# Hybrid decoder layer, fp32 weights in two halves: the halves of some stages start at other bytes of SBUF

## Chip, cores and metric

The kernel runs on one core of one Trainium2 chip. The metric is the device time of one execution in microseconds (us); the median before is 1079.64 us, from two runs of 1079.58 and 1079.71.

## What is computed

One layer on 256 tokens of width 2048, all in float32. Cut to what matters here:

```python
h   = rmsnorm(x)
z   = h @ w_in          # pool channels | q | k | v | indexer q | indexer k | indexer weights
A   = pool_mixer(z)     # four groups, causal means over 2, 4, 8, 16 tokens, a small matmul each
B   = dsa_attention(z)  # 16 indexer heads, causal top-64 keys, 8 heads of softmax attention
x1  = x + concat(A, B) @ w_out                     # 2048 x 2048
up  = rmsnorm(x1) @ w_up                           # 2048 x 11264
out = x1 + (silu(gate(conv3(up))) * val(conv3(up))) @ w_down    # 5632 x 2048
```

## The kernel before, in words

**Two halves.** To reach float32 accuracy with the fast fp32r matmul, every operand is split into a high and a low half, and each product is three matmuls: high by high, high by low, low by high (`mm_tok`, L225 to L227, and `mm_feat`, L231 to L233). The weights stream in as pieces of 1 MB units (`raw`, two buffers). For each piece of 1024 columns ScalarE rounds `raw` into `whi` (L118) and VectorE subtracts it into `wlo` (L119); `whi` and `wlo` have four buffers each. The activations are held in halves for a whole stage: `xhl` (normalised input), `yhl` (mixer output), `x2hl` (second norm, in the memory of `xhl`) and `ghl` (FFN gate product).

**Stages.** TensorE goes through one list of 384 pieces. First the columns of `w_in` in chunks in the order of `ORDER`: indexer chunks i0, i1, i2, key k0, k1, pool u0, query q0, q1, u1, value v0, u2, v1, u3. Then `w_out` (32 pieces), `w_up` (176 pieces) and `w_down` (88 pieces). In the token chunks (i, k, q, v: `tok_chunk`, `mm_tok`) the activation slice of 128 tokens is the stationary operand and the weights are the moving one, of 400, 384, 320 or 512 columns. In the pool chunks and in everything after (`mm_feat`) it is the other way round: 128 columns of weight halves are stationary and the 256 tokens of an activation half move. The four pool chunks have 384 such matmuls (96 each); k, q and v have six chunks of 96 matmuls of 512 columns; `w_out` has 768, `w_up` 4224, `w_down` 2112, which is 264 for each eighth (11 pieces of 24).

**Side work.** Indexer scores, top-k, attention heads, pooling and norms are put between the pieces by a table of steps (`at(step, f)`): before piece n's matmuls the units of piece n+3 are loaded, piece n+2 is split, and the side functions of step n are recorded. The order on each engine is then that of the recording, but for instructions that wait for a buffer: such a one is put behind what frees it. Head h's probabilities are transposed into `pT` (L528, five buffers) at step 60+3h and used in `att_pv` at step 74+h for heads 0 to 3, and later for 4 to 7. The sums for the second norm are kept in `sq1` (L610, own memory); `ffn_open` (L631) closes the memory pool of the mixer and opens that of the FFN at step G0+1; `r2.cols` (L167) and `r2.rows` (L178) are the small matmuls of the second norm.

**Where the operands lie.** The starts of the tiles, in bytes of a partition, are fixed in the compiled program. A stationary weight slice is 128 columns of 4 bytes, 512 bytes; a moving activation half is 1,024 bytes and a moving slice of 512 columns 2,048. So in a stage the remainder of an operand's start by 512 bytes is the same for every matmul, and this text counts it in steps of 64 bytes, as a **place** from 0 to 7. Before: `whi` and `wlo` all start at multiples of 512 (91,648 and so on): place 0. `xhl` starts at 34,560: place 4. `x2hl` is 448 bytes further: place 3. `yhl` (136,832 and 64 of offset) and `ghl` (124,416 and 192): place 3. The offsets are those of `PLACE` (L45, in elements of 4 bytes). The **distance** of a stage is the place of the moving operand less that of the stationary one, modulo 8:

| stage | moving | stationary | distance before | after |
|---|---|---|---|---|
| i0, first and second slice of a piece | weights 0 and 1 | xhl 4 | 4 and 5 | 4 and 5 |
| i1, both slices | weights 0 | xhl 4 | 4 | 4 |
| i2, first and second slice | weights 0 and 4 | xhl 4 | 4 and 0 | 4 and 0 |
| k0, k1, q0, q1, v0, v1 | weights | xhl 4 | 4, all six | 7, 1, 2, 6, 3, 5 |
| u0 to u3 | xhl 4 | weights | 4 | 3 |
| w_out, w_up | yhl, x2hl 3 | weights 0 | 3 | 3 |
| w_down, eighths 0 to 7 | ghl 3 | weights | 3, all eight | 3, 2, 1, 0, 7, 6, 5, 4 |

(The second slice of a piece of i0 starts 1,600 bytes in, of i2 1,280.)

Of the kernel before, what the change touches and what calls it, by code (L numbers as in the profile page):

```python
# [8 lines left out]
F32 = mybir.dt.float32  # L9
F32R = mybir.dt.float32r  # L10
BF16 = mybir.dt.bfloat16
# [4 lines left out]
P = 128  # L16
S = 256
# [19 lines left out]
GROUPS = (3, 2, 1, 0)  # L37

ORDER = ("i0", "i1", "i2", "k0", "k1", "u0", "q0", "q1", "u1", "v0", "u2", "v1", "u3")
WARM = 8  # L40

PLACE = {"x": 0, "x2": 112, "y": 16, "g": 48}  # L45


def placed(pool, n, name, o, of=None):

    m = n * 2 * S  # L50
    t = of[0] if of else pool.tile([P, m + (128 if name == "xhl" else o)], F32R, name=name)
    return t, t[:, o:o + m].rearrange("p (k a t) -> p k a t", k=n, a=2)
# [3 lines left out]
def hybrid_kernel(ctx, tc, xT, par, wIa, wIb, wIc, wI2, wA, wU, wP, wO, wUp, wDn, out):  # L56
    nc = tc.nc
    PS = bass.MemoryType.PSUM

    cp = ctx.enter_context(tc.tile_pool(name="cp", bufs=1))  # L60
    wp = ctx.enter_context(tc.tile_pool(name="wp", bufs=2))
# [5 lines left out]

    xhl = placed(cp, KT, "xhl", PLACE["x"])
    x2hl = placed(cp, KT, "xhl", PLACE["x2"], xhl)
    xhl, x2hl = xhl[1], x2hl[1]  # L70
    ga = cp.tile([P, KT], F32, name="ga")


    warm = cp.tile([P, 512], BF16, name="warm")
    nc.vector.memset(warm, 0.0)
    pw = ps_s.tile([P, 512], F32, name="pw", tag="ss")
    for i in range(WARM):
        nc.tensor.matmul(pw, warm[:, 0:P], warm, start=True, stop=True)

    ident = cp.tile([P, P], F32, name="ident")  # L80
    make_identity(nc, ident)
# [9 lines left out]
    class Unit:  # L91


        def __init__(self, src, n, cuts=None):
            self.src, self.n, self.raw, self.cuts = src, n, None, cuts or [(0, n)]
# [10 lines left out]
    class Piece:  # L106


        def __init__(self, unit, a, b, mm):
            self.unit, self.a, self.b, self.mm = unit, a, b, mm  # L110

        def split(self, parts=1):
            self.hi = wp.tile([P, 1024], F32R, name="whi", tag="whi", bufs=4)
            self.lo = wp.tile([P, 1024], F32R, name="wlo", tag="wlo", bufs=4)
            n = (self.b - self.a) // parts
            for c in range(0, n * parts, n):
                raw, hi = self.unit.raw[:, self.a + c:self.a + c + n], self.hi[:, c:c + n]
                i1 = nc.scalar.activation(hi, raw, AF.Copy)  # L118
                i2 = nc.vector.tensor_tensor(self.lo[:, c:c + n], raw, hi.bitcast(F32), op=ALU.subtract)  # L119
                self.issued = i1.ins, i2.ins  # L120
# [4 lines left out]
    pieces = []  # L125
    sides = {}

    def at(step, f, *a):
        sides.setdefault(step, []).append(lambda: f(*a))
# [12 lines left out]
    zc = zp.enter_context(tc.tile_pool(name="zc", bufs=1))  # L142
# [42 lines left out]
    r1, r2 = TokenNorm("r1"), TokenNorm("r2")  # L185
# [31 lines left out]
    def mm_tok(acc, piece, ks, width):  # L217

        pt = acc.get()
        for i, k in enumerate(ks):  # L220
            wh, wl = piece.get(i * width, width)
            for th in range(2):
                t = slice(th * P, (th + 1) * P)
                o = pt[:, th, :width]
                nc.tensor.matmul(o, xhl[:, k, 0, t], wh, start=(k == 0), stop=False)  # L225
                nc.tensor.matmul(o, xhl[:, k, 0, t], wl, start=False, stop=False)  # L226
                nc.tensor.matmul(o, xhl[:, k, 1, t], wh, start=False, stop=(k == KT - 1))  # L227

    def mm_feat(o, wh, wl, rhs, first, last):

        nc.tensor.matmul(o[:, 0:S], wh, rhs[:, 0], start=first, stop=False)  # L231
        nc.tensor.matmul(o[:, 0:S], wh, rhs[:, 1], start=False, stop=False)  # L232
        nc.tensor.matmul(o[:, 0:S], wl, rhs[:, 0], start=False, stop=last)  # L233

    def tok_chunk(srcs, width, cuts=()):

        acc = Acc()
        for q in range(4):
            u = Unit(srcs[q], 4 * width, cuts[q] if q < len(cuts) else None)
            for h in range(2):  # L240
                def mm(p, k0=4 * q + 2 * h):
                    mm_tok(acc, p, (k0, k0 + 1), width)
                pieces.append(Piece(u, 2 * h * width, (2 * h + 2) * width, mm))
        return acc


    def pool_chunk(n):
        acc = Acc()
        for j in range(2):
            u = Unit(wU[2 * n + j], D)  # L250
            for h in range(2):
                def mm(p, j=j, h=h):
                    pt = acc.get()
                    for i in range(8):
                        k = 8 * h + i
                        mm_feat(pt[:, j], *p.get(i * P, P), xhl[:, k], k == 0, k == KT - 1)
                pieces.append(Piece(u, h * 1024, (h + 1) * 1024, mm))
        return acc

    ia, za, ua, first = [], {}, [], {}  # L260
    W = IWIDTH[0]

    def pair_chunk():

        accs = Acc(), Acc()
        seq = [(0, 0), (0, 1)] + [cm for m in range(6) for cm in ((1, m), (0, m + 2))] + [(1, 6), (1, 7)]
        for j in range(8):
            n = [2 * IWIDTH[c] for c, m in seq[2 * j:2 * j + 2]]
            src = wIa if j == 0 else wIc if j == 7 else wIb[j - 1]
            u = Unit(src, sum(n), [(0, W), (W, 2 * W), (2 * W, 4 * W)] if j == 0 else  # L270
                     [(0, n[0]), (n[0], sum(n))] if j < 4 else None)
            for i in range(2):
                def mm(p, c=seq[2 * j + i][0], m=seq[2 * j + i][1]):
                    mm_tok(accs[c], p, (2 * m, 2 * m + 1), IWIDTH[c])
                pieces.append(Piece(u, n[0] * i, n[0] + n[1] * i, mm))
        ia.extend(accs)

    for name in ORDER:
        first[name] = len(pieces)
        if name == "i0":  # L280
            pair_chunk()
        elif name == "i1":
            first[name] = first["i0"] + 8
        elif name == "i2":
            ia.append(tok_chunk([wI2[q] for q in range(4)], IWIDTH[2]))
        elif name[0] == "u":
            ua.append(pool_chunk(int(name[1])))
        else:
            c = ("k0", "k1", "q0", "q1", "v0", "v1").index(name)
            za[name] = tok_chunk([wA[c, q] for q in range(4)], 512)  # L290


    yhl = placed(zc, KT, "yhl", PLACE["y"])[1]
    oa = [Acc() for g in range(8)]
# [26 lines left out]
    G0 = len(pieces)  # L321
# [16 lines left out]
    for i in range(16 * NF // 8):  # L338
        if i % 2 == 0:
            u = Unit(wDn[i // 2], 2048)  # L340

        def mm(p, i=i):
            for n in range(8):
                t, k = divmod(8 * i + n, NF)
                if t < 14:
                    mm_feat(da[t // 2].get()[:, t % 2], *p.get(n * P, P), ghl[:, k], k == 0, k == NF - 1)
                else:
                    mm_feat(da[t - 7].get(), *p.get(n * P, P), ghl[:, k], k == 0, k == NF - 1)
        o = (i % 2) * 1024
        pieces.append(Piece(u, o, o + 1024, mm))  # L350


    qiT = [zc.tile([P, 8, S], F32R, name=f"qiT{c}", tag="big", bufs=2) for c in range(2)]
# [169 lines left out]
    def att_pt(h):  # L523
        pe = hs[h]
        tp = ps_s.tile([P, 512], F32, name="tp", tag="ss")
        for i in range(3):
            nc.tensor.transpose(tp[:, i * P:(i + 1) * P], pe[:, i * P:(i + 1) * P], ident)  # L527
        pT = zc.tile([P, 3 * P], F32, name="pT", tag="pT", bufs=5)  # L528
        nc.scalar.activation(pT, tp[:, 0:3 * P], AF.Copy)
        hs[h] = pT  # L530

# [75 lines left out]
                                           op0=ALU.mult, op1=ALU.subtract)  # L607


    sq1 = cp.tile([P, 2, S], F32, name="sq1")  # L610

    def x1_out(jp):
        pt = oa[jp].get()
        x1 = xf[:, 2 * jp:2 * jp + 2]
        nc.vector.tensor_tensor(x1, pt[:, :, 0:S], x1, op=ALU.add)
        for j in range(2):
            split_x(2 * jp + j, x1[:, j], pr[:, C_FG:C_FG + KT], True, x2hl)
        if jp == 0:
            nc.scalar.activation(sq1, x1, AF.Square)
        else:  # L620
            t = zc.tile([P, 2, S], F32, name="xt", tag="t2", bufs=5)
            nc.scalar.activation(t, x1, AF.Square)
            nc.vector.tensor_tensor(sq1, sq1, t, op=ALU.add)
# [7 lines left out]
    def ffn_open():  # L631
        nonlocal ghl
        zp.close()
        fp = ctx.enter_context(tc.tile_pool(name="fp", bufs=1))
        ghl = placed(fp, NF, "ghl", PLACE["g"])[1]
        fw["up"] = [fp.tile([P, 2, S + 2], F32, name=f"up{i}") for i in range(2)]
# [82 lines left out]
        at(st + 2 + 4 * (n < 3), pool_mix, n)  # L719
    for jp in range(8):  # L720
        at(O0 + 4 * jp + 4, x1_out, jp)
    at(G0 + 1, ffn_open)
    at(G0 + 1, sq1_sum)
    at(G0 + 2, r2.cols, sq1[:, 0])
    at(G0 + 3, r2.diag)
    at(G0 + 4, r2.rows)
    for f in range(NF):
# [104 lines left out]
```

## Time and profile before

| | |
|---|---|
| median of two runs | 1079.64 us |
| the profiled execution | 1079.61 us |
| its span, first to last instruction | 1077.9 us |
| TensorE matmuls busy | 1072.1 us (99%), 8644 matmuls |
| TensorE weight loads busy | 1042.4 us (97%) |
| VectorE, ScalarE, GpSimd busy | 697.0, 544.9, 13.8 us |
| mean granted clock of TensorE | 0.999 |

Matmuls overlap in the profile: one of 256 columns is shown with some 277 ns, but the next starts long before that. So the **spacing**, the time from a matmul's start to the next one's, is what tells how fast the stream runs. It is read from the start times in the timeline, over 12 or more matmuls, since a start is shown to 10 ns.

### The profile page before, as it was taken

What the parts mean: (1) busy time and instruction counts of PE and PEld (TensorE: products, weight loads), DVE (VectorE), ACT (ScalarE), POOL (GpSimd) and SP (SyncE); (2) the same over time, 40 slices, a digit from 0 to 9 for tenths busy, and PEclk for the clock granted to TensorE, in tenths of its full rate; (3) what the DMA queues carried; (4) which work ended last, traced back from release to release, by engine and by line L of the source; (5) the groups of instructions that cost most, each with busy time, mean ns of one, the idle gap of its engine ahead of it and who ended that gap; (6) DMA issues with size and microseconds to landing.
All of it is one profiled execution on the core that took longest, in us unless ns stands there. A gap on an engine that the chain in (4) does not pass through costs nothing.

```text
span 1077.9 us, 20309 instructions
## 1 busy us (share of the span) xinstructions
PE 1072.1 (99%) x8644; PEld 1042.4 (97%) x8644; DVE 697.0 (65%) x986; ACT 544.9 (51%) x745; POOL 13.8 (1%) x25
## 2 busy tenths in 40 slices
PE   9999999999999999999999999999999999999998
PEld 7988989889999999999999999999999999999998
DVE  7667857765566676777777777777676544444443
ACT  7655356654545555555555555555555433333342
POOL 0001000000000000000000000000000000000000
PEclk9999999999999999999999999999999999999999
DMA  8553554444555455555555555555555555556552
GB/s 288 174 180 144 194 209 156 165 167 157 194 192 192 168 199 195 194 193 196 196 195 196 196 196 196 195 196 195 188 197 187 196 204 199 203 200 204 203 207 85
DMA packets 31770, 204.55 MB, mean 190 GB/s; under 512 B 3648, under 2 KB 4288, under 8 KB 8640
## 3 DMA queue, kind: packets, MB, share of 16 engines
q1 hardware_dynamic: 30240, 201.16, 52.9%
q10 hardware_dynamic: 1440, 2.11, 0.5%
q8 instruction: 67, 1.10, 0.4%
q14 instruction: 23, 0.19, 0.0%
HBM read 201.15 MB, written 2.10 MB: 189 GB/s over the span
## 4 chain that ended last, share of the span: by engine, by line
PE 99%; DMA 1%; SPq 0%; ACT 0%; DVE 0%; issue 0%; ACTq 0%
PE mm L233 26%; PE mm L231 26%; PE mm L232 26%; PE mm L225 6%; PE mm L227 5%; PE mm L226 5%; PE sp L413 1%; DMA xf<-in_xT_dram 1%; PE sp L499 0%; PE tp L487 0%; PE op L539 0%; PE tp L527 0%; PE tp L403 0%; PE pm L232 0%; PE pm L233 0%; PE pm L231 0%
## 5 line engine op out<-in xcount | busy, mean ns | idle before, releaser
L119 DVE TENSOR_TENSOR wlo<-raw,whi 128x1024 fp32r<-128x1024 f32 (+4 forms) x385 | 462.3, 1203 | 293.0 <-ACT whi L118 289.1
L118 ACT ACTIVATE whi<-raw 128x1024 fp32r<-128x1024 f32 (+4 forms) x385 | 400.0, 1042 | 434.6 <-PE mm L232 305.9
L231 PE MATMUL mm<-xhl,whi 128*128 128x256 f32 x1536 | 426.1, 277 | 0.0
L233 PE MATMUL mm<-xhl,wlo 128*128 128x256 f32 x1536 | 424.9, 277 | 0.0
L232 PE MATMUL mm<-xhl,whi 128*128 128x256 f32 x1536 | 424.9, 277 | 0.0
L232 PEld LDWEIGHTS mm<-xhl,whi 128*128 128x128 f32 x1536 | 288.9, 188 | 0.2
L231 PEld LDWEIGHTS mm<-xhl,whi 128*128 128x128 f32 x1536 | 288.8, 188 | 0.2
L233 PEld LDWEIGHTS mm<-xhl,wlo 128*128 128x128 f32 x1536 | 288.8, 188 | 0.0
L231 PE MATMUL mm<-ghl,whi 128*128 128x256 f32 x704 | 194.3, 276 | 0.0
L232 PE MATMUL mm<-ghl,whi 128*128 128x256 f32 x704 | 194.3, 276 | 0.0
L233 PE MATMUL mm<-ghl,wlo 128*128 128x256 f32 x704 | 194.3, 276 | 0.0
L231 PEld LDWEIGHTS mm<-ghl,whi 128*128 128x128 f32 x704 | 132.2, 188 | 0.0
L232 PEld LDWEIGHTS mm<-ghl,whi 128*128 128x128 f32 x704 | 132.2, 188 | 0.0
L233 PEld LDWEIGHTS mm<-ghl,wlo 128*128 128x128 f32 x704 | 132.2, 188 | 0.0
L225 PE MATMUL mm<-whi,xhl 128*128 128x512 f32 (+3 forms) x288 | 108.6, 377 | 1.0 <-ACT xhl L135 0.8
L226 PE MATMUL mm<-wlo,xhl 128*128 128x512 f32 (+3 forms) x288 | 106.6, 370 | 0.2 <-DVE wlo L119 0.2
L227 PE MATMUL mm<-whi,xhl 128*128 128x512 f32 (+3 forms) x288 | 106.7, 370 | 0.0
L231 PE MATMUL mm<-yhl,whi 128*128 128x256 f32 x256 | 70.8, 277 | 0.0
L232 PE MATMUL mm<-yhl,whi 128*128 128x256 f32 x256 | 70.7, 276 | 0.0
L233 PE MATMUL mm<-yhl,wlo 128*128 128x256 f32 x256 | 70.7, 276 | 0.0
L225 PEld LDWEIGHTS mm<-whi,xhl 128*128 128x128 f32 x288 | 54.2, 188 | 9.4 <-ACT xhl L135 1.1
L227 PEld LDWEIGHTS mm<-whi,xhl 128*128 128x128 f32 x288 | 54.1, 188 | 8.4 <-DVE xhl L138 0.5
(144 smaller groups left out, 751.9 us busy)
## 6 DMA issues: line engine op xcount, KB each, us to landing
raw<-in_wUp_dram SPq DMA_DIRECT2D x88, 1024.0 KB, 4.8
raw<-in_wDn_dram SPq DMA_DIRECT2D x44, 1024.0 KB, 4.8
raw<-in_wA_dram SPq DMA_DIRECT2D x24, 1024.0 KB, 4.8
raw<-in_wO_dram SPq DMA_DIRECT2D x16, 1024.0 KB, 4.8
raw<-in_wU_dram SPq DMA_DIRECT2D x8, 1024.0 KB, 4.8
raw<-in_wI_dram SPq DMA_DIRECT2D x4, 640.0 KB, 3.9
raw<-in_wIb_dram SPq DMA_DIRECT2D x3, 784.0 KB, 4.4
xf<-in_xT_dram SPq DMA_DIRECT2D x8, 256.0 KB, 5.1
```

The source lines that it names most:

```text
L118: i1 = nc.scalar.activation(hi, raw, AF.Copy)
L119: i2 = nc.vector.tensor_tensor(self.lo[:, c:c + n], raw, hi.bitcast(F32), op=ALU.subtract)
L225: nc.tensor.matmul(o, xhl[:, k, 0, t], wh, start=(k == 0), stop=False)
L226: nc.tensor.matmul(o, xhl[:, k, 0, t], wl, start=False, stop=False)
L227: nc.tensor.matmul(o, xhl[:, k, 1, t], wh, start=False, stop=(k == KT - 1))
L231: nc.tensor.matmul(o[:, 0:S], wh, rhs[:, 0], start=first, stop=False)
L232: nc.tensor.matmul(o[:, 0:S], wh, rhs[:, 1], start=False, stop=False)
L233: nc.tensor.matmul(o[:, 0:S], wl, rhs[:, 0], start=False, stop=last)
L413: nc.tensor.matmul(sp[:, a:b], q, kiT[:, e, 0:b - a], start=(e == 0), stop=(e == 1))
```

## The change

It gives each `Piece` an offset in elements. `whi` and `wlo` become 512 bytes wider, and the piece uses 1024 columns from its offset on. The offset is 16 elements (64 bytes) times a number: 1 in the pool columns; 3, 5, 6, 2, 7, 1 in k0, k1, q0, q1, v0, v1; 0 to 7 in the eighths of `w_down`; 0 in the indexer chunks, `w_out` and `w_up`. The memory for it (eight tiles by 512 bytes) comes from three places: `sq1` moves into the rotating buffers "t2" of the mixer's pool, for which `ffn_open` is recorded behind `r2.cols`; `pT` has four buffers for five; and the tile of the warm-up matmuls is half as wide, with 16 matmuls of 256 columns for 8 of 512. In the program that comes of it, all activation tiles keep their places (`yhl` starts 1,536 bytes later, `ghl` too), and so do the small ones that TensorE reads, but for `sq1`, which goes from place 6 to place 0.

```diff
-WARM = 8
+WARM = 16
+PAD = 128
...
-    warm = cp.tile([P, 512], BF16, name="warm")
+    warm = cp.tile([P, 256], BF16, name="warm")
...
-        nc.tensor.matmul(pw, warm[:, 0:P], warm, start=True, stop=True)
+        nc.tensor.matmul(pw[:, 0:256], warm[:, 0:P], warm, start=True, stop=True)
...
-        def __init__(self, unit, a, b, mm):
-            self.unit, self.a, self.b, self.mm = unit, a, b, mm
+        def __init__(self, unit, a, b, mm, off=0):
+            self.unit, self.a, self.b, self.mm, self.off = unit, a, b, mm, off
...
-            self.hi = wp.tile([P, 1024], F32R, name="whi", tag="whi", bufs=4)
-            self.lo = wp.tile([P, 1024], F32R, name="wlo", tag="wlo", bufs=4)
+            self.hi = wp.tile([P, 1024 + PAD], F32R, name="whi", tag="whi", bufs=4)[:, self.off:self.off + 1024]
+            self.lo = wp.tile([P, 1024 + PAD], F32R, name="wlo", tag="wlo", bufs=4)[:, self.off:self.off + 1024]
...
-                pieces.append(Piece(u, h * 1024, (h + 1) * 1024, mm))
+                pieces.append(Piece(u, h * 1024, (h + 1) * 1024, mm, 16))
...
-            za[name] = tok_chunk([wA[c, q] for q in range(4)], 512)
+            za[name] = tok_chunk([wA[c, q] for q in range(4)], 512, off=16 * (3, 5, 6, 2, 7, 1)[c])
...
-        pieces.append(Piece(u, o, o + 1024, mm))
+        pieces.append(Piece(u, o, o + 1024, mm, 16 * (i // 11)))
...
-        pT = zc.tile([P, 3 * P], F32, name="pT", tag="pT", bufs=5)
+        pT = zc.tile([P, 3 * P], F32, name="pT", tag="pT", bufs=4)
...
-    sq1 = cp.tile([P, 2, S], F32, name="sq1")
+    sq1 = None
...
+        if jp == 0:
+            sq1 = zc.tile([P, 2, S], F32, name="sq1", tag="t2", bufs=5)
...
-    at(G0 + 1, ffn_open)
     at(G0 + 1, sq1_sum)
-    at(G0 + 2, r2.cols, sq1[:, 0])
+    at(G0 + 2, lambda: r2.cols(sq1[:, 0]))
+    at(G0 + 2, ffn_open)
```

With four buffers, the fifth head's `pT` needs the buffer of the first head's, which is read by that head's `att_pv`. On ScalarE, at the end of chunk v0, the rows before are these (`whi` are the splits, `pT_2140` is head 4's, `pe` the exponentials of head 5, `zv` the values leaving PSUM):

```order
L490 ACTIVATE qk_2114<-tp_2109,gqk_110 128x256
L491 ACTIVATE qk_2114<-tp_2109 128x256
L455 ACTIVATE zv_2133<-mm_1886,r1_429 128x512 x2
L529 ACTIVATE pT_2140<-tp_2136 128x384
L118 ACTIVATE whi_2183<-raw_2099 128x1024
L511 ACTIVATE pe_2152,sume_2153<-sm_2145,nb_2150,sc1_1832 128x128
L511 ACTIVATE pe_2152,sume_2153<-sm_2145,nb_2150,sc1_1832 128x256
L118 ACTIVATE whi_2211<-raw_2181 128x1024
```

After, head 4's is `pT_2147`:

```order
L492 ACTIVATE qk_2121<-tp_2116,gqk_118 128x256
L493 ACTIVATE qk_2121<-tp_2116 128x256
L457 ACTIVATE zv_2140<-mm_1893,r1_436 128x512 x2
L120 ACTIVATE whi_2190<-raw_2106 128x1024
L513 ACTIVATE pe_2159,sume_2160<-sm_2152,nb_2157,sc1_1839 128x128
L513 ACTIVATE pe_2159,sume_2160<-sm_2152,nb_2157,sc1_1839 128x256
L120 ACTIVATE whi_2218<-raw_2188 128x1024
L120 ACTIVATE whi_2269<-raw_2188 128x1024
L531 ACTIVATE pT_2147<-tp_2143 128x384
```

Head 4's `pT` has moved behind two splits and the exponentials; nothing else on ScalarE has moved. On VectorE one small product (`nb`) changes places with its neighbour, and on TensorE nothing moves but the warm-up.

## Rows read from the trace of the kernel before

**Rows 1.** The page: busy time of the engines, and the granted clock in 40 slices.
```profile
PE 1072.1 (99%) x8644; PEld 1042.4 (97%) x8644; DVE 697.0 (65%) x986; ACT 544.9 (51%) x745; POOL 13.8 (1%) x25
...
PEclk9999999999999999999999999999999999999999
```
**Rows 2.** Stretches: length, busy (count) of PE, PEld, DVE, ACT, POOL, clock, DMA, GB/s.
```profile
112.00:124.00 12.00, 12.00 (x100) 11.92 (x99) 10.17 (x27) 6.29 (x9) 1.64 (x1) 1.00 0.49 175
500.00:600.00 100.00, 100.00 (x885) 100.00 (x884) 72.72 (x105) 53.98 (x74) 0.00 (x0) 1.00 0.55 191
900.00:1000.00 100.00, 100.00 (x885) 100.00 (x884) 46.83 (x41) 39.32 (x37) 0.00 (x0) 1.00 0.59 204
```
**Rows 3.** Timeline of TensorE (start us, us, line): 12 matmuls of u0.
```profile
122.23 0.28 PE L231 MATMUL mm<-xhl,whi 128*128 128x256 f32 x1
...
123.67 0.40 PE L225 MATMUL mm<-whi,xhl 128*128 128x512 f32 x1
```
**Rows 4.** The same in w_out, 12 matmuls.
```profile
311.71 0.28 PE L231 MATMUL mm<-yhl,whi 128*128 128x256 f32 x1
...
313.07 0.28 PE L231 MATMUL mm<-yhl,whi 128*128 128x256 f32 x1
```
**Rows 5.** Line 231 alone, first and eighth eighth of w_down: count, first and last start.
```profile
L231 PE MATMUL mm<-ghl,whi x88: 276/276/276, 835.1 to 864.7; 128*128 128x256 f32 x88
...
L231 PE MATMUL mm<-ghl,whi x87: 276/276/276, 1044.9 to 1074.1; 128*128 128x256 f32 x87
```
**Rows 6.** Timeline of TensorE in k1, steady: 12 matmuls.
```profile
99.92 0.39 PE L225 MATMUL mm<-whi,xhl 128*128 128x512 f32 x1
...
102.64 0.39 PE L225 MATMUL mm<-whi,xhl 128*128 128x512 f32 x1
```
**Rows 7.** Timeline of TensorE in i0: six matmuls of each slice of a piece.
```profile
17.97 0.34 PE L225 MATMUL mm<-whi,xhl 128*128 128x400 f32 x1
...
19.05 0.34 PE L225 MATMUL mm<-whi,xhl 128*128 128x400 f32 x1
...
20.14 0.34 PE L225 MATMUL mm<-whi,xhl 128*128 128x384 f32 x1
```
**Rows 8.** The same in i2.
```profile
47.76 0.31 PE L225 MATMUL mm<-whi,xhl 128*128 128x320 f32 x1
...
48.64 0.31 PE L225 MATMUL mm<-whi,xhl 128*128 128x320 f32 x1
...
49.53 0.33 PE L413 MATMUL sp<-kiT,qiT 128*128 128x128 f32 x2
```
**Rows 9.** Timeline of TensorE in k0, behind indexer scores (L413): six matmuls.
```profile
68.79 0.40 PE L225 MATMUL mm<-whi,xhl 128*128 128x512 f32 x1
...
70.18 0.40 PE L225 MATMUL mm<-whi,xhl 128*128 128x512 f32 x1
```
**Rows 10.** Timeline of TensorE in w_up, around the small matmuls of the norm.
```profile
361.47 0.28 PE L231 MATMUL mm<-xhl,whi 128*128 128x256 f32 x1
...
366.66 0.28 PE L233 MATMUL mm<-xhl,wlo 128*128 128x256 f32 x1
366.78 0.61 PE L178 MATMUL pb<-dg,ones 128*128 128x128 f32 x4
```
**Rows 11.** Timeline at the end of v0 and in u2: head 4's pT, heads 0 and 5.
```profile
212.30 0.49 ACT L529 ACTIVATE pT<-tp 128x384 f32<-128x384 f32 x1
...
217.82 1.06 ACT L118 ACTIVATE whi<-raw 128x1024 fp32r<-128x1024 f32 x1 [1.83 <-PE mm L232]
...
218.11 0.38 PE L540 MATMUL op<-pT,zv 128*128 128x128 f32 x2
...
222.29 0.49 PE L527 MATMUL tp<-ident,pe 128*128 128x128 f32 x3
```
**Rows 12.** Timeline of the start: warm-up, and what the third real matmul waits for.
```profile
1.25 3.60 PE L78 MATMUL pw<-warm 128*128 128x512 bf16 x8 [1.25 <-DVE warm L75]
...
5.42 0.19 PEld L227 LDWEIGHTS mm<-whi,xhl 128*128 128x128 f32 x1 [0.25 <-DVE xhl L138]
```

More of the change, by code (lines that the diff above doesn't have):

```diff
@@ L233, in mm_feat, with tok_chunk @@
         nc.tensor.matmul(o[:, 0:S], wl, rhs[:, 0], start=False, stop=last)
-    def tok_chunk(srcs, width, cuts=()):
+    def tok_chunk(srcs, width, cuts=(), off=0):
         acc = Acc()
@@ L242, in mm @@
                     mm_tok(acc, p, (k0, k0 + 1), width)
-                pieces.append(Piece(u, 2 * h * width, (2 * h + 2) * width, mm))
+                pieces.append(Piece(u, 2 * h * width, (2 * h + 2) * width, mm, off))
         return acc
@@ L607, in pool_mix @@
                                            op0=ALU.mult, op1=ALU.subtract)
-    sq1 = cp.tile([P, 2, S], F32, name="sq1")
+    sq1 = None
     def x1_out(jp):
+        nonlocal sq1
+        if jp == 0:
+            sq1 = zc.tile([P, 2, S], F32, name="sq1", tag="t2", bufs=5)
         pt = oa[jp].get()
```

## The prediction
> **What bounds the kernel now.** I read the page's list of engines first: TensorE's matmuls fill 1072.1 us of a span of 1077.9, at the full granted clock of 2.4 GHz in nearly all of it, while VectorE and ScalarE have 65% and 51% [rows 1]. So only what changes TensorE's own stream can change the time. The table by stretch comes next, and what to see in it is that the stream does not care how busy the others are: with VectorE at 73 us of 100 and at 47 us of 100 the same 885 matmuls touch a stretch [rows 2]. That leaves the spacing of the matmuls. A matmul of 256 columns at 2.4 GHz has 256 / 2.4 = 106.7 ns of columns to stream, one of 512 has 213.3.
>
> The timeline gives the spacings. In the pool chunk u0, 12 matmuls take 123.67 - 122.23 = 1.44 us, 120.0 ns each [rows 3]. In `w_out` the same 12 take 1.36 us, 113.3 ns each [rows 4], and in `w_down` 261 matmuls take 29.6 us in the first eighth and 258 take 29.2 in the last, 113.4 and 113.2 ns [rows 5]. The instructions have the same shapes, and VectorE's load was just ruled out; what differs is the distance of moving and stationary operand: 4 in the pool chunks, 3 in the others. So distance 4 costs 13.3 ns over the columns and distance 3 costs 6.7, half of it.
>
> In the token chunks the roles are exchanged. In k1 the spacing is 2.72 us / 12 = 226.7, 13.3 over the columns, at distance 4 [rows 6]. i0 has two distances in each piece: six matmuls of 400 columns take 1.08 us at distance 4 (180.0 each, 13.3 over) and 1.09 at distance 5 (181.7, 15.0 over) [rows 7]. i2 has distances 4 and 0: 0.88 and 0.89 us for six of 320 columns, some 147 to 148 each, 13 to 15 over [rows 8]. So with the roles exchanged 4 and 0 cost the same as 4 in the pool chunks, and 5 no less. Distances 1, 2, 6 and 7 are shown nowhere, in either role.
>
> **The change part by part.** The profiled execution took 1079.61 us, 1.71 more than its span and 0.03 under the median, so sums on it are sums on the median.
>
> *Pool columns.* All 384 matmuls go from distance 4 to 3: 384 x (120.0 - 113.3) = 2.56 us less [rows 3, 4]. This is the term I trust most, since w_out shows the same kind of matmul at the new distance.
>
> *Key, query, value chunks.* 96 matmuls in each, so one step of 6.7 ns is worth 0.64 us in a chunk. v0 comes to distance 3: if what holds in `w_out` holds with the roles exchanged, -0.64. v1 comes to 5, which i0 shows 1.7 ns dearer than 4: +0.16 [rows 7]. k0, k1, q0, q1 come to 7, 1, 2, 6, unseen: from -0.64 (as distance 3) to +0.46. The upper end is the dearest spacing that rows of these chunks show, behind an interruption: 1.39 us for six, 231.7 ns, 5 over the steady 226.7, times 96 = 0.48 [rows 9]. As the nearer rows give 4, 0 and 5 all alike, I take -0.32 for each of the four, halfway to distance 3: -1.28. Sum of the six: -1.76; ends -3.84 (all as good as 3) and +2.9 (all as dear as rows 9).
>
> *w_down.* 264 matmuls in each eighth, so a step of 6.7 ns is worth 1.76 us. Eighth 0 stays as it is. Eighth 7 comes to distance 4, which u0 shows: +1.76. Eighths 1 to 6 come to 2, 1, 0, 7, 6, 5. The nearest rows at both sides are the two steady levels of this shape, 113.3 and 120.0; 0 and 5 are dear with the roles exchanged [rows 7, 8], 1, 2, 6, 7 are open. I take the middle, +0.88 each, +5.28 together. Sum +7.04. The ends: nothing can go under 106.7 ns of columns, so no eighth gains more than 1.76, so six such gains and the +1.76 of eighth 7 make -8.8; all seven at 120 make +12.3.
>
> *The rest costs nothing that ends anything.* `whi` and `wlo` are written and read by the same instructions of the same sizes on ScalarE and VectorE, which have a third and a half of the span free [rows 1]. With a buffer less, head 4's `pT` waits for head 0's last matmul, at 218.11 + 0.38 = 218.49 instead of running at 212.30; ScalarE is then in a split until 218.88, so `pT` ends near 219.4. What is behind it on ScalarE, a `yhl` and a `qk`, comes 0.4 us later; the first matmul that can need the freed PSUM buffer is head 5's transpose at 222.29, so 2.9 us of cover are left [rows 11]. Without that cover it would cost the wait itself, at most the 6.9 us by which `pT` moves. The warm-up has the same 4,096 columns and ends where the third real matmul still waits for VectorE at 5.42 [rows 12]. `sq1` and the later `ffn_open` touch VectorE, ScalarE and GpSimd only.
>
> *Sum:* -2.56 - 1.76 + 7.04 = +2.7 us, 1079.6 + 2.7 = 1082.3 us.
>
> *A rule that speaks against all of it.* The rows show a spacing that goes with the place of the operands [rows 3, 4]. The Trainium skill, "TensorE: Matmul & The Clock Gate", Step-by-step: what each phase is for, has two independent SBUF read ports for TensorE, so that loading the next weights takes no bandwidth from the running matmul; "SBUF — State Buffer", Who interferes with whom, adds that TensorE never waits on anyone. By that rule no place matters; it is the first rival. The Trainium skill, "TensorE: Matmul & The Clock Gate", Back-to-back issue gap, gives 256 / 2.4 + 2.5 = 109.2 ns as the spacing of such a matmul alone; no stretch here reaches it, and if a distance did, an eighth would gain 1.1 us by that estimate.
>
> **The rivals.**
>
> *No place matters* (the rule above). Then u0's 120 has another reason, for example its neighbours in the side work, every term is 0, and the time is 1079.6. For it: the pool chunks are also the ones with pooling and attention between their pieces. Against it: within 12 matmuls without any side work the spacing is steady at 120 [rows 3], and k1 shows the same 13.3 ns without pool columns [rows 6].
>
> *Only distance 4 is dear, all the others are as good as 3.* Then pool -2.56, k to v -3.84, w_down +1.76: -4.6, 1075.0. For it: 3 is good right beside 4. Against it: 0 and 5 in i2 and i0 are as dear as 4 [rows 7, 8].
>
> *Distance 3 is the only good one.* Pool -2.56, v0 -0.64, w_down +12.3: +9.1, 1088.7. For it: i0 and i2. Against it: those have the roles exchanged.
>
> *A slow rhythm sets in for good; slower by over 2%.* At distance 3 there is a second rhythm. From 361.47 to 366.66 the spacing is 5.19 us over 44 matmuls, 118.0 ns, behind the norm's small matmuls, and it lasts until the next of these at 366.78, behind which it is 113.3 to the end [rows 10, 5]. Here `sq1` has another place and the offsets come on top; if the stream falls into this rhythm behind the second small matmul (366.78) instead, nothing interrupts it any more. The remaining 4224 - 96 = 4128 matmuls of `w_up` and 2112 of `w_down` would pay 4.7 ns: +29.3, less 2.56: 1106.3, +2.5%. It decides at one point, the first matmuls behind 366.78. Against it: there the addresses and the order are those of before.
>
> **How the numbers follow.** Mixture of the two levels, my forecast, 1082.3: 0.50, with a range of its own from 1077 to 1087. No place matters, 1079.6: 0.12. Only 4 is dear, 1075.0: 0.15. Only 3 is good, 1088.7: 0.19. Slow rhythm, 1106.3: 0.04. The range reaches from just under the 1075.0 to just over the 1088.7 and leaves out the slow rhythm and the gains below both levels: 1074.5 to 1090. Against the bound of 2%, 21.6 us, about what a measurement of this kernel can tell from no change, only the slow rhythm is slower: 0.04. Faster by that much would need every matmul of `w_down`, k, q and v at the bare columns and more: 0.01. Within: 0.95.
>
> **What would show it right or wrong.** In the profile after: u0 at 113.3 ns a matmul; v0 at 220 for 512 columns; eight stretches of `w_down` with different spacings, from 29.9 us (113.3) to 31.7 us (120.0) each, the last at 31.7; the spacing in `w_out` and `w_up` unchanged at 113.3; no gap of TensorE at 218 to 223 us. Wrong if u0 stays at 120 (then place is not it), if all eighths are alike, if a spacing lies outside 106.7 to 120, or if `w_up` runs at 118 behind 367 us.

## The result, and the profile after

The changed kernel takes 1088.13 us (two runs, 1088.01 and 1088.25) against 1079.64: a ratio of 1.0078, interval 1.0062 to 1.0094. It is 0.8% slower, within the 2% that the forecast called no change, and within its range of 1074.5 to 1090; the forecast itself, 1082.3, is 5.8 us too low.

The profiled execution after took 1088.01 us, with a span of 1086.3 (1077.9 before). The page's list of engines and the granted clock, for [rows 1]:

```profile
PE 1081.1 (100%) x8652; PEld 1050.8 (97%) x8652; DVE 696.3 (64%) x986; ACT 545.5 (50%) x745; POOL 13.7 (1%) x25
...
PEclk9999999999999999999999999999999999999999
```

TensorE's busy time grew by 9.0 us, with VectorE and ScalarE within 0.7 us of before, and the clock is still 2.4 GHz. The eight added matmuls are those of the warm-up (16 halves for 8). So the same matmuls stand further apart. The next view is the one that answers to [rows 5]: line 233 of the changed kernel (line 231 before) alone, in each eighth of `w_down`. Columns: count, shortest, median and longest duration in ns, first and last start in us.

```profile
L233 PE MATMUL mm<-ghl,whi x88: 276/276/276, 834.8 to 864.4; 128*128 128x256 f32 x88
...
L233 PE MATMUL mm<-ghl,whi x88: 276/281/285, 864.7 to 895.7; 128*128 128x256 f32 x88
...
L233 PE MATMUL mm<-ghl,whi x88: 279/279/284, 896.0 to 926.8; 128*128 128x256 f32 x88
...
L233 PE MATMUL mm<-ghl,whi x88: 280/283/287, 927.1 to 958.4; 128*128 128x256 f32 x88
...
L233 PE MATMUL mm<-ghl,whi x88: 276/276/279, 958.8 to 988.4; 128*128 128x256 f32 x88
...
L233 PE MATMUL mm<-ghl,whi x87: 280/283/287, 1051.2 to 1082.1; 128*128 128x256 f32 x87
```

The first five and the last are shown. Read from first start to first start: 29.9, 31.3, 31.1, 31.7, then 29.9 again, and the last has the durations and the length of the fourth. The sixth and seventh have 31.3 and 31.1 us. The eighths repeat after four: 113.4, 118.6, 117.8, 120.0 ns a matmul at distances 3, 2, 1, 0, and the same four again at 7, 6, 5, 4. (Mean spacings of a stretch, here and below, are worked out from the starts of all matmuls in it.)

In the token chunks the spacing of 512 columns grew. The timeline of TensorE after (start us, us, line, operation), 12 matmuls each of k0 (distance 7) and k1 (1); k1 answers to [rows 6]:

```profile
86.11 0.39 PE L227 MATMUL mm<-whi,xhl 128*128 128x512 f32 x1
...
88.90 0.33 PE L415 MATMUL sp<-kiT,qiT 128*128 128x128 f32 x2
...
99.25 0.39 PE L227 MATMUL mm<-whi,xhl 128*128 128x512 f32 x1
...
101.99 0.39 PE L227 MATMUL mm<-whi,xhl 128*128 128x512 f32 x1
```

That is 2.79 / 12 = 232.5 and 2.74 / 12 = 228.3 ns, where [rows 6] have 226.7 at distance 4. The steady spacing in the chunks is 233.4 in k0 (7), 233.3 in v0 (3), 228.6 in k1 (1), 228.9 in v1 (5), and 232 to 233.4 in q0 and q1 (2 and 6). Before, the chunks were not at 226.7 throughout: behind each piece of side work the spacing took some eight matmuls to settle there. Over the matmuls of k0 that follow one another directly it was 229.7 on the mean and is 233.0 now, so a chunk pays less than the steady spacings alone would make.

Last, twelve matmuls each of u0, of `w_out` and of `w_up` behind the norm, for [rows 3], [rows 4] and the end of [rows 10]:

```profile
121.50 0.28 PE L233 MATMUL mm<-xhl,whi 128*128 128x256 f32 x1
...
122.86 0.28 PE L233 MATMUL mm<-xhl,whi 128*128 128x256 f32 x1
...
299.86 0.28 PE L233 MATMUL mm<-yhl,whi 128*128 128x256 f32 x1
...
301.22 0.28 PE L233 MATMUL mm<-yhl,whi 128*128 128x256 f32 x1
...
367.63 0.28 PE L233 MATMUL mm<-xhl,whi 128*128 128x256 f32 x1
...
368.99 0.28 PE L233 MATMUL mm<-xhl,whi 128*128 128x256 f32 x1
```

1.36 us in each, 113.3 ns: u0 came down from 120.0, the two stages that the change leaves alone stayed. By stage, from first start to the next stage's first start, the change is (us):

| stage | forecast | measured |
|---|---|---|
| i0 to i2 | 0 | -0.51 |
| u0, u1, u2, u3 | -0.64 each: -2.56 | -0.61, -0.35, -0.36, -0.56: -1.88 |
| k0, k1, q0, q1, v0, v1 | -0.32 four times, -0.64, +0.16: -1.76 | +0.33, +0.15, +0.48, +0.48, +0.42, +0.08: +1.94 |
| w_out, w_up | 0 | 0.0, 0.0 (89.28 and 479.85 in both) |
| w_down, eighths 0 to 7 | 0, six times +0.88, +1.76: +7.04 | 0.00, +1.40, +1.18, +1.77, +0.01, +1.40, +1.18, +1.76: +8.70 |
| sum | +2.7 | +8.25 |

The first real matmul starts 0.17 us later in this execution; 8.2 + 0.17 is the 8.4 us of the spans. The i chunks depend on when the first data come: over executions of kernels in which nothing differs there they went from -0.51 to +0.59, so nothing is read from them.

### The profile page after: what moved, and what is told of

It is laid out like the page before. It is cut to its first block, busy times and chain, and to the rows that moved or that the text cites. A ratio compares the mean times of both kernels' runs of the same rounds, so it can differ in the third digit from the quotient of the medians.

```text
span 1086.3 us, 20328 instructions
## 1 busy us (share of the span) xinstructions
PE 1081.1 (100%) x8652; PEld 1050.8 (97%) x8652; DVE 696.3 (64%) x986; ACT 545.5 (50%) x745; POOL 13.7 (1%) x25
## 4 chain that ended last, share of the span: by engine, by line
PE 99%; DMA 0%; DVE 0%; ACT 0%; SPq 0%; issue 0%; ACTq 0%
PE mm L234 26%; PE mm L233 26%; PE mm L235 26%; PE mm L229 6%; PE mm L228 6%; PE mm L227 6%; PE sp L415 1%; PE sp L501 0%; DMA raw<-in_wIa_dram 0%; PE tp L489 0%; PE op L541 0%; PE tp L529 0%; PE tp L405 0%; PE pm L233 0%; PE pm L234 0%; PE pm L235 0%
## 5 line engine op out<-in xcount | busy, mean ns | idle before, releaser
L234 PE MATMUL mm<-ghl,whi 128*128 128x256 f32 x704 | 197.2, 280 | 0.0
L233 PE MATMUL mm<-ghl,whi 128*128 128x256 f32 x704 | 197.0, 280 | 0.0
L235 PE MATMUL mm<-ghl,wlo 128*128 128x256 f32 x704 | 197.0, 280 | 0.0
```

## The experiments

The questions: is it the place at all, and not another edit; what the period is (the forecast counted in 512 bytes); which access is slowed; and why u1 and u2 gained less than u0. Diffs are against the changed kernel.

### All offsets back to nothing, other edits kept

```diff
-                pieces.append(Piece(u, h * 1024, (h + 1) * 1024, mm, 16))
+                pieces.append(Piece(u, h * 1024, (h + 1) * 1024, mm, 0))
...
-    za[name] = tok_chunk(..., off=16 * (3, 5, 6, 2, 7, 1)[c])
+    za[name] = tok_chunk(..., off=0)
...
-        pieces.append(Piece(u, o, o + 1024, mm, 16 * (i // 11)))
+        pieces.append(Piece(u, o, o + 1024, mm, 0))
```

> All offsets 0, the wider tiles, the smaller warm-up tile, the four pT buffers and sq1 in the rotating buffers kept. Theory (all of the change is the distance of the operands): back to the time before, 1079.6 us within 0.5, pool chunks at 120.0 ns a matmul, every eighth of w_down 29.9 us. Rival (the wider tiles, the later pT or the warm-up cost something): 1080.5 or more, with the extra time outside w_down.

Measured: 1079.77 us against 1079.55, a ratio of 1.0000 (0.9990 to 1.0009). Behind the i chunks every stage has the length of before to 0.01 us: u0 11.51, k0 27.01, each eighth 29.92. So the wider tiles, the warm-up, the buffer less of `pT` and `sq1` cost nothing, and all that happened comes from the offsets.

### Only the pool columns shifted, twice

The second and third edit of the above, with the 16 of the pool columns kept.

> Only the pool columns shifted by 64 bytes. Theory (as the changed kernel's stages read): the pool chunks 1.9 us shorter and nothing else, 1077.7 us, all eighths of w_down 29.9 us. Rival (the chunks beside them gave or took part of it): the pool chunks another sum than -1.9, by 0.5 us or more; the sum forecast was -2.56, 1077.1 us.

> Only the pool columns shifted, once more and with more rounds, as the version that should beat both kernels. Theory (the pool chunks' spacing alone): 1.3 us less than before by the stages of its first profile, a ratio of 0.9988. Rival (no gain that a measurement tells): the interval holds 1.

Measured: 1078.34 against 1079.55, 0.9987 (0.9978 to 0.9997), and again 1078.28 against 1079.40, 0.9988 (0.9979 to 0.9997). This beats the kernel before by 0.1%, twice with an interval that leaves out 1, and the changed kernel by 0.9%. The pool chunks gained 0.21, 0.36, 0.37 and 0.36 us in the first, 1.3 together, where the changed kernel has 1.88 from the same addresses. So the 1.9 of the first expectation was missed, and its rival, another sum, held. u0 shows it; line 233 of u0, the changed kernel first:

```profile
L233 PE MATMUL mm<-xhl,whi x32: 276/276/285, 112.3 to 122.9; 128*128 128x256 f32 x32
```

and this kernel:

```profile
L233 PE MATMUL mm<-xhl,whi x32: 281/281/281, 112.3 to 123.3; 128*128 128x256 f32 x32
```

31 times three matmuls in 10.6 and in 11.0 us, 114.0 and 118.3 ns. The address of every operand of u0 is the same in both; what differs is what ran before it (k0 and k1 with other places). So at one and the same distance the stream has two rhythms (steady patterns of spacing), 113.3 and 117.8. The longer one is that of [rows 10]. In the changed kernel u0 and u3 run at 113.3, u1 and u2 at 117.8 in their first two pieces and 113.3 in the other two; in this kernel three of the four chunks have two such pieces, and u0 has four. Even two executions of this kernel differ: u1 took 12.74 us in one and 12.55 in the other.

### `ghl` one place further

```diff
-PLACE = {"x": 0, "x2": 112, "y": 16, "g": 48}
+PLACE = {"x": 0, "x2": 112, "y": 16, "g": 64}
```

The eighths now have distances 4, 3, 2, 1, 0, 7, 6, 5.

> The changed kernel with ghl 64 bytes later, at place 4, so that the eighths of w_down have distances 4, 3, 2, 1, 0, 7, 6, 5 for 3, 2, 1, 0, 7, 6, 5, 4. Theory (spacing goes by the distance modulo 256 bytes, 4 places): the pattern moves on by one eighth: 120.0, 113.3, 118.6, 117.8, 120.0, 113.3, 118.6, 117.8 ns, so 31.7, 29.9, 31.3, 31.1 us twice; the sum of w_down grows by under 0.1 us, as each of the four comes twice again: 1088.1 us. Rival (the place of the weights alone decides): the pattern stays, 29.9, 31.3, 31.1, 31.7 twice.

Measured: 1090.63 us. Line 233 in the first six eighths:

```profile
L233 PE MATMUL mm<-ghl,whi x88: 280/283/283, 835.1 to 866.4; 128*128 128x256 f32 x88
...
L233 PE MATMUL mm<-ghl,whi x88: 281/281/281, 866.8 to 897.5; 128*128 128x256 f32 x88
...
L233 PE MATMUL mm<-ghl,whi x88: 279/281/285, 897.9 to 928.8; 128*128 128x256 f32 x88
...
L233 PE MATMUL mm<-ghl,whi x88: 280/280/280, 929.2 to 959.9; 128*128 128x256 f32 x88
...
L233 PE MATMUL mm<-ghl,whi x88: 280/283/283, 960.3 to 991.6; 128*128 128x256 f32 x88
...
L233 PE MATMUL mm<-ghl,whi x88: 281/281/281, 991.9 to 1022.7; 128*128 128x256 f32 x88
```

The long eighths (31.7 us) moved with the distance: the first and the fifth, 4 and 0. Distances 2 and 6 cost 1.41 us, 1 and 5 cost 1.17, as in the changed kernel, so it is the difference of the two places that counts and the period is four places, 256 bytes. A miss is in it: distances 3 and 7 (second and sixth eighth) were to be at 113.3 and stand at 117.8. That is the second rhythm again, or a place of `ghl` that matters by itself; the last experiment decides. Distance 1, too, stands at 117.8 here and in the changed kernel, the number of the second rhythm. It was always entered from distance 2 or from that rhythm, so no run tells whether its 117.8 is the price of the place or the rhythm.

### Only the low halves shifted

```diff
...
-            self.lo = wp.tile(...)[:, self.off:self.off + 1024]
+            self.lo = wp.tile(...)[:, self.off_lo:self.off_lo + 1024]
...
-        pieces.append(Piece(u, o, o + 1024, mm, 16 * (i // 11)))
+        pieces.append(Piece(u, o, o + 1024, mm, 0, 16 * (i // 11)))
```

In `w_down` two of each three matmuls stay at distance 3, and only the third (`wlo`) goes through 3, 2, 1, 0, 7, 6, 5, 4.

> In w_down whi stays at place 0 and only wlo is shifted, by 0 to 7 places in the eighths. The three matmuls of a weight slice stand at lines 233, 234, 235 (high-high, high-low, low-high). Theory (the loading of the next weights collides with the running matmul's moving operand): the spacing from line 234 to line 235, in which wlo is loaded, takes the distances 3, 2, 1, 0, 7, 6, 5, 4 and is longer by 4 to 7 ns in six eighths, the other two spacings stay at 113.3; an eighth is 29.9 us or some 30.3 to 30.5, the whole 1079.6 - 1.9 + 1.9 + 8.7 / 3 = 1082.5 us. Rival (a matmul collides with its own weights): the spacing behind line 235 is the longer one. Second rival (the rhythm of three settles as a whole): all three grow alike.

Measured: 1085.65 us; the eighths change by 0.00, +1.29, +0.02, +1.16, +1.17, +1.29, +0.03, +1.16. This kernel has one line more, so the three matmuls, at 233 to 235 in the expectation, are at lines 234, 235 and 236. Line 234 (high by high), whose operands did not move, in the first five:

```profile
L234 PE MATMUL mm<-ghl,whi x88: 276/276/276, 835.0 to 864.6; 128*128 128x256 f32 x88
...
L234 PE MATMUL mm<-ghl,whi x88: 276/283/286, 864.9 to 895.8; 128*128 128x256 f32 x88
...
L234 PE MATMUL mm<-ghl,whi x88: 276/276/281, 896.1 to 925.7; 128*128 128x256 f32 x88
...
L234 PE MATMUL mm<-ghl,whi x88: 276/281/281, 926.1 to 956.8; 128*128 128x256 f32 x88
...
L234 PE MATMUL mm<-ghl,whi x88: 281/281/281, 957.1 to 987.9; 128*128 128x256 f32 x88
```

The time is not paid at the matmul whose weights moved. In the second eighth the spacings behind lines 234, 235 and 236 are 119.0, 119.5 and 116.1 ns, in the fourth 117.4, 118.3 and 117.6. So of the three expectations the last, that the three grow together, is nearest. The length is not a sum of a price for each matmul either: one of the three at distance 2 costs 1.29 us, all three there cost 1.40. `wlo` at distance 1 or 5 costs nothing if the other two are at 3, though all three at 1 cost 1.18 us.

Three of the eighths tell less than they seem to. In eighth 4 `wlo` is at distance 7, which the eighths of the changed kernel have shown to be as good as 3, and still the spacing is 117.8: that is the second rhythm. Eighths 3 and 7 have 117.75 as well, so their +1.16 may be that rhythm and no price of distances 0 and 4. Which access stands in the way of which isn't settled by this.

### A map in steps of 8 bytes

`w_up`'s output tile f at 8f bytes for f below 32 and back at 0 from there, pieces of `w_down` alternating between offset 0 and others, the pieces of the token chunks at multiples of 32 bytes.

```diff
-            pieces.append(Piece(us[j], h * 1024, (h + 1) * 1024, mm))
+            pieces.append(Piece(us[j], h * 1024, (h + 1) * 1024, mm, 2 * f if f < 32 else 0))
...
-        pieces.append(Piece(u, o, o + 1024, mm, 16 * (i // 11)))
+        pieces.append(Piece(u, o, o + 1024, mm, 0 if i % 4 < 2 else (4 * (i // 4) if i < 64 else 0)))
...
-                pieces.append(Piece(u, 2 * h * width, (2 * h + 2) * width, mm, off))
+                pieces.append(Piece(u, 2 * h * width, (2 * h + 2) * width, mm, off * (2 * q + h)))
...
-    za[name] = tok_chunk(..., off=16 * (3, 5, 6, 2, 7, 1)[c])
+    za[name] = tok_chunk(..., off=8)
```

> A map in one profile, read stretch by stretch and not by its time: in w_up the weights' offset grows by 8 bytes with every output tile (0 to 248 bytes in tiles 0 to 31, then 0), in w_down pairs of pieces at offset 0 alternate with pairs at 0, 16, ... 240 bytes, and the pieces of the k, q and v chunks stand at 0, 32, ... 224 bytes. Theory (distance modulo 256 bytes, with the two rhythms): w_up starts at 113.3 ns and passes 118, 118, 120 at offsets 64, 128, 192 as the eighths of w_down did; between them no spacing above 120.5 or under 106.7; w_down's pairs at offset 0 come back to 113.3. Rival (only steps of 64 bytes matter): the spacing changes only at multiples of 64 bytes. For k, q, v: offset 0 stays the best, 226.7 ns, and 64, 128, 192 give 229, 232 and 233.

Measured: 1100.23 us. Twelve matmuls each of the tiles at 24 and at 216 bytes in the timeline:

```profile
396.09 0.28 PE L233 MATMUL mm<-xhl,whi 128*128 128x256 f32 x1
...
397.45 0.28 PE L233 MATMUL mm<-xhl,whi 128*128 128x256 f32 x1
...
667.00 0.28 PE L233 MATMUL mm<-xhl,whi 128*128 128x256 f32 x1
...
668.47 0.28 PE L233 MATMUL mm<-xhl,whi 128*128 128x256 f32 x1
```

113.3 and 122.5 ns. Places finer than 64 bytes count. In `w_up` 8 bytes give 118.4, 16 give 118.7, 24 give 113.3, 32 give 117.3, 40 give 120.0, 48 give 119.8, 64 give 118.6, 192 give 120.0. The tile at 216 bytes has 121.8 over its whole length, above the bound that was expected, and nothing lies under 113.3. The tiles from 32 on, back at 0, run at 113.3.

In `w_down` twelve of the sixteen pairs at offset 0 run at 113.3, as expected; four, those behind the pairs at 112, 192, 208 and 224 bytes, stand at 117.8. Line 233 in the pair at 0 behind 144 bytes, and in the one behind 192:

```profile
L233 PE MATMUL mm<-ghl,whi x16: 276/276/277, 962.5 to 967.6; 128*128 128x256 f32 x16
...
L233 PE MATMUL mm<-ghl,whi x16: 281/281/281, 995.8 to 1001.1; 128*128 128x256 f32 x16
```

45 spacings in 5.1 and in 5.3 us. So a change of place, with nothing in between, can choose the rhythm too. And 32 bytes give 120.0 in `w_down` where they give 117.3 in `w_up`: the numbers of the map hold for the order in which it was gone through.

In the token chunks offset 0, distance 4, settles to the shortest spacing of the eight (227; 230 where side work interrupts), with some 229 at 64 bytes next and some 232 to 234.5 at the rest. So the place of before was already the best one there, and in `w_up` none is better than it.

### What sets the rhythm: interruptions

Pool columns alone shifted, all of `w_down` at distance 3, and 1, 2, ... 6 extra matmuls of one column in float32 (into a free PSUM buffer that nothing reads) behind the first piece of eighths 1, 2, ... 6.

```diff
+    def poke(n):
+        pk = ps_s.tile([P, 512], F32, name="pk", tag="ss")
+        for q in range(n):
+            nc.tensor.matmul(pk[:, q:q + 1], ident, ones[:, 0:1], start=True, stop=True)
...
+    for e in range(1, 7):
+        at(D0 + 11 * e + 1, poke, e)
```

> Pool columns shifted, all other offsets 0, so all of w_down is at distance 3; one to six extra matmuls of one column (of ones and the identity, into a PSUM tile that nobody reads) interrupt the stream once in each of the eighths 1 to 6. Theory (at distance 3 there are two rhythms, and what ran before chooses): behind at least one of the six the spacing stays at some 117.8 ns until the next, that eighth takes some 31.1 us and not 29.9 with the 0.3 to 0.9 us of the interruption. Rival (addresses alone decide, 118 comes from the small matmuls of the norm or a neighbour): 113.3 within ten matmuls behind each of them, every eighth 30.2 to 30.8 us.

Measured: 1087.63 us. Line 233 between the interruptions, behind 1, 2, 3, 4, 5 and 6 of them:

```profile
L233 PE MATMUL mm<-ghl,whi x88: 276/276/372, 866.5 to 896.2; 128*128 128x256 f32 x88
...
L233 PE MATMUL mm<-ghl,whi x88: 281/281/364, 896.9 to 927.8; 128*128 128x256 f32 x88
...
L233 PE MATMUL mm<-ghl,whi x87: 276/276/279, 929.1 to 958.4; 128*128 128x256 f32 x87
...
L233 PE MATMUL mm<-ghl,whi x88: 281/281/364, 959.5 to 990.4; 128*128 128x256 f32 x88
...
L233 PE MATMUL mm<-ghl,whi x88: 276/276/365, 991.7 to 1021.4; 128*128 128x256 f32 x88
...
L233 PE MATMUL mm<-ghl,whi x146: 281/281/281, 1023.5 to 1074.7; 128*128 128x256 f32 x146
```

Behind 1, 3 and 5 the stream has 113.35 ns, behind 2, 4 and 6 it has 117.75, at once and until the next interruption, the last one to the kernel's end. Whether the number decides or the rhythms only take turns is open: here both say the same.

The next kernel has 2, 1, 2, 2, 1, 1 of them, at the same six points (step D0 + 11e + 12 for e from 0 is D0 + 11e + 1 for e from 1):

```diff
+    for e, n in enumerate((2, 1, 2, 2, 1, 1)):
+        at(D0 + 11 * e + 12, poke, n)
```

> As the run with one to six interrupting matmuls, but 2, 1, 2, 2, 1, 1 of them in the eighths 1 to 6, all of w_down at distance 3. Theory A (an even number turns the rhythm round, an odd number sets the fast one; it fits the six of before and the two groups of four matmuls of the norm): slow 117.8, fast 113.3, slow, fast, fast, fast. Theory B (an even number sets the slow rhythm, an odd one the fast): slow, fast, slow, slow, fast, fast. Rival (the moment of the interruption decides, not the number): some other row of six.

Measured: 1084.36 us. Line 233 between the interruptions:

```profile
L233 PE MATMUL mm<-ghl,whi x88: 281/281/364, 867.2 to 898.1; 128*128 128x256 f32 x88
...
L233 PE MATMUL mm<-ghl,whi x88: 276/276/365, 898.6 to 928.2; 128*128 128x256 f32 x88
...
L233 PE MATMUL mm<-ghl,whi x88: 281/281/364, 929.0 to 959.8; 128*128 128x256 f32 x88
...
L233 PE MATMUL mm<-ghl,whi x88: 281/281/364, 960.5 to 991.3; 128*128 128x256 f32 x88
...
L233 PE MATMUL mm<-ghl,whi x88: 276/276/365, 991.8 to 1021.5; 128*128 128x256 f32 x88
...
L233 PE MATMUL mm<-ghl,whi x153: 276/276/372, 1022.0 to 1073.8; 128*128 128x256 f32 x153
```

Slow, fast, slow, slow, fast, fast. An even number sets the slow rhythm, whatever it was, and an odd one the fast one. If the rhythms took turns, or an even number turned over what it found, the stretch behind the fourth would be fast; it is slow, and the sixth is fast behind fast. That is 12 interruptions of 12 in the two kernels. The moment doesn't decide: four of the six points had an odd number in one kernel and an even one in the other, and the rhythm went with the number. The norm's two one-column matmuls ahead of the stretch of [rows 10] fit it (two, slow). Those of L178 at its end don't fit the count alone: two of 128 columns, and the rhythm behind them is fast. So the number of short matmuls sets it for one column, and what sets it in general stays open.

### The same with `ghl` one place further

`ghl` at place 4 as above, with one such matmul behind the first piece of eighths 1 and 5, which have distances 3 and 7.

```diff
-PLACE = {"x": 0, "x2": 112, "y": 16, "g": 48}
+PLACE = {"x": 0, "x2": 112, "y": 16, "g": 64}
...
+    for e in (1, 5):
+        at(D0 + 11 * e + 1, poke, 1)
```

> The changed kernel with ghl at place 4, and one interrupting matmul of one column behind the first piece of the eighths 1 and 5, which are at distances 3 and 7. Theory (their 117.8 ns in the run without it was the slow rhythm, and what ran before had set it): 113.3 ns behind the interruption, these two eighths 30.2 to 30.5 us each for 31.1. Rival (the good distance goes with the absolute place of an operand, ghl at 3): they stay at 117.8 ns, 31.1 us and a little.

Measured: 1088.81 us, 1.8 less than without the interruptions. Line 233 over the whole of eighth 1 and of eighth 5 (the extra matmul comes behind the first of the 11 pieces):

```profile
L233 PE MATMUL mm<-ghl,whi x88: 276/276/363, 866.6 to 896.5; 128*128 128x256 f32 x88
...
L233 PE MATMUL mm<-ghl,whi x88: 276/276/363, 990.9 to 1020.7; 128*128 128x256 f32 x88
```

Behind the interruption it is 113.35 ns in both. In eighth 1 it was 117.8 until then. Eighth 5 had some 113.4 from its first piece on, behind the change from distance 0, where the kernel without extra matmuls came out at 117.8; so only eighth 1 tests the interruption. The two eighths now cost 0.35 and 0.23 us instead of 1.18 each, the extra matmul included. So distances 3 and 7 are good wherever `ghl` lies, and what the earlier kernel paid there was the slow rhythm.

## Why the prediction was right or wrong

**Right: what bounds it, and by what it moves.** TensorE's spacing alone made the difference, and the offsets made the spacing; with them gone all is as before. (The place is not all of it: at one place the stream has two rhythms.) The first rival, that no place matters, has fallen: one kernel has spacings of 113.4, 117.8, 118.6 and 120.0 ns for one and the same instruction. The Trainium skill, "TensorE: Matmul & The Clock Gate", Step-by-step: what each phase is for, and "SBUF — State Buffer", Who interferes with whom, has it that loading weights takes nothing from the running matmul and that TensorE waits on nobody. The spacings of this trace don't agree with the reading of it by which no place matters; which access waits for which, no run shows.

**Right: the parts at nothing, u0, and eighth 7.** u0 came to 113.3 and eighth 7 cost 1.76, to the hundredth what was forecast from [rows 3] and [rows 4]. `w_out` and `w_up` kept their lengths. `pT` behaved as worked out from [rows 11]; the timeline after, with ScalarE's split, `pT` behind it, and the next matmuls of TensorE around them:

```profile
218.28 1.06 ACT L120 ACTIVATE whi<-raw 128x1024 fp32r<-128x1024 f32 x1 [0.88 <-PE mm L234]
...
218.58 0.38 PE L542 MATMUL op<-pT,zv 128*128 128x128 f32 x2
...
219.25 0.47 ACT L531 ACTIVATE pT<-tp 128x384 f32<-128x384 f32 x1
...
222.40 0.38 PE L542 MATMUL op<-pT,zv 128*128 128x128 f32 x2
```

`pT` ends at 219.72 (forecast 219.4), and TensorE has no gap there. Two slips of that paragraph cost nothing: the 6.9 us by which `pT` was to move is 6.6 in [rows 11] (212.30 to 218.88), and `sq1` is read by TensorE too, in the norm's small matmuls.

**Wrong: key, query and value.** The step that failed is "if what holds in `w_out` holds with the roles exchanged, -0.64", and with it "halfway to distance 3" for the four unseen ones. With the weights moving, 3 and 7 are the worst (233.3 and 233.4 ns, with 2 and 6 hardly better) and 4 is the best (226.7); 0 was met at 320 columns alone, where it costs the same as 4 [rows 8]. The sum is +1.94 for -1.76, 3.7 us of the error of 5.8. The upper end given, +2.9 from [rows 9], held: 231.7 there is close to what the bad distances have all the time. The one place taken from a row of this same role, v1 from [rows 7], had +0.16 forecast and +0.08 measured; k1, at distance 1 and so at the same one modulo 4, has +0.15.

**Wrong: distance counted modulo 8.** The step is "in steps of 64 bytes, as a place from 0 to 7", with the remainder by 512 bytes. The spacing repeats after 256 bytes, in both roles. So eighth 4, put at +0.88, cost 0.01 and is the equal of eighth 0, and eighth 3 is the equal of eighth 7. [rows 8], in which distances 0 and 4 cost the same, could have told it, and were read as "0 and 5 are dear".

**Mis-sized: the six middle eighths.** "I take the middle, +0.88 each" stood for two levels, 113.3 and 120.0, with nothing known between. There are two more, 117.8 and 118.6 (the first perhaps the second rhythm, as said). The six cost 6.94 us, 1.16 each, and `w_down` +8.70 for +7.04.

**Mis-sized: the pool columns.** The -2.56, "the term I trust most", came out at -1.88, mainly since u1 and u2 run half their pieces at 117.8. The mechanism of the last rival, the slow rhythm, is real and struck here, in pieces between the side work, and not behind 366.78, where it would have cost 29 us.

**Of the rivals** "only 3 is good", 1088.7, is nearest to the time, but by errors that cancel: 7 is just as good as 3, v0 lost where it was to gain, and its distances 1, 2, 5 and 6 cost two thirds to four fifths of what 4 does. A look at the stages, and not the total, shows that. The measured 1088.13 lies in the range only because the range was drawn out to this rival; it is 1.1 us over the 1077 to 1087 that the forecast's own mixture was given.

## What to carry to other kernels

Where TensorE is full and each matmul loads its weights, read the spacing by stage from start to start: the places of the two operands, modulo 256 bytes here, were worth 3% of it at 512 columns and 7% at 256 (226.7 to 234, 113.3 to 121.8). What was measured in one role of the operands is not to be taken over to the other, and the places of a kernel whose stages all stand at the best spacing seen are better left alone. A change of rhythm at unchanged addresses is looked for behind short matmuls, and behind a stretch at other addresses.

## What the runs showed that was not expected

- With 128 columns of weights loaded for each matmul in fp32r, 256 moving columns have spacings from 113.3 to 121.8 ns, by the starts of the operands, in steps finer than 64 bytes (8 bytes: 113.3 to 118.4). With 512 columns they go from 226.7 to some 234.
- At the same addresses there are two steady rhythms, 113.35 and 117.75 ns; which of the two is set by the last interruption or change of place, and lasts until the next. Behind an even number of one-column float32 matmuls it was the slow one and behind an odd number the fast one, 12 times of 12; behind other side work two executions of one and the same kernel can differ (u1). In the trace one such float32 matmul is shown as two records. The timeline of TensorE in the first kernel with extra matmuls has the two behind the first piece of eighth 2 as four:

```profile
896.58 0.50 PE L746 MATMUL pk<-ones,ident 128*128 128x1 f32 x4
```

- A matmul at a bad distance slows its neighbours too: with only the low halves moved, to distance 2, the spacings behind the three lines were 119.0, 119.5 and 116.1 ns, the last behind the one that had moved. Whether accesses collide and which, and why one short matmul more or less in an interruption matters, stays open.
